# Conditioning rows by sums along the free axis, weights packed by tile, norms summed by a full matrix

## The chip, the cores and the metric

The kernel runs on one core of a Trainium2 chip. The metric is the device time of one execution in microseconds. Three runs of the kernel before took 2370.89, 2377.98 and 2380.05 us; their median is 2377.98 us.

## The reference

Two layers, each a mixer (eight heads of differential attention and eight heads of windowed grouped-query attention with a sink, side by side) and a squared-ReLU MLP, on 256 tokens of width 2048. Every sub-layer is modulated by a conditioning vector `c`:

```python
c_act = silu(c)
for layer in range(2):
    mod = c_act @ ada_w[layer] + ada_b[layer]           # 2048 -> 6 * 2048
    sh1, sc1, g1, sh2, sc2, g2 = split(mod, 6)
    h = rmsnorm(x, norm_mix[layer]) * (1 + sc1) + sh1
    proj = h @ w_in[layer]                              # 2048 -> 4608: qa, ka, va, qb, kb, vb
    ... two attentions ...
    x = x + g1 * (concat(out_a, out_b) @ w_out[layer])  # 2048 -> 2048
    h2 = rmsnorm(x, norm_mlp[layer]) * (1 + sc2) + sh2
    x = x + g2 * (square(relu(h2 @ w_up[layer])) @ w_down[layer])   # 2048 -> 8192 -> 2048
return rmsnorm(x, final_norm)
```

All is float32. `ada_w` alone has 201 MB, the other weights 377 MB, and each is read once.

## The kernel before

The activations stay in SBUF, transposed: `X[i]` holds two chunks of 128 features (partitions) by 256 tokens. Every weight comes from HBM as a tile `raw` of 512 KB (128 partitions x 1024 elements). ScalarE rounds it to `whi` (line 354, a cast to float32r), VectorE forms the rest `wlo = raw - whi` (line 355), and TensorE multiplies both with the two halves of the activation (lines 395 and 397 for most, 364 to 368 and 411 for others), so that a product is made of three, hi by hi, hi by lo and lo by hi. Layer 0's first pair of chunks stays whole (line 364).

The conditioning rows are a matrix-vector product of 201 MB, and VectorE makes it: `ada_job` loads tiles `araw` with the 2048 inputs on the partitions, 16 groups of 128 one after the other, multiplies each by its 128 values of `c_act` (one scalar a partition) and adds it to a running sum `ada` (lines 204 and 206, a `scalar_tensor_tensor` over 1024 columns). The 128 partitions of the sum are still to be added up: TensorE transposes it by the identity (line 213) and ScalarE copies each 128x128 block with `accum_out` (line 215); small VectorE operations add the bias and the norm's gain (lines 222, 225). One job makes up to eight rows of 128 values at once, after 16 groups.

`araw` and `raw` share one pool of six buffers of 512 KB (`rawp`). All loads stand on one queue, SyncE's, in the order of the program, and a load waits there until the buffer that it takes is free, that is until VectorE is done with the tile that lay in it. The `ada` tiles are dealt out between the weight tiles by `feed(rate)`, with rates in the tables `R0` to `R3`; `need` loads whatever is still missing when a row is used. A scheduler fixes the order on every engine before the run.

Around each sub-layer stands a norm. `square_sum` squares `X[i]` on ScalarE and sums over the partitions on TensorE with `mean_d`, a column of 1/2048, as the right operand (line 529, 16 matmuls with one column each); `rstd_cols` makes the reciprocal root of 2x128 values in nine small ScalarE operations (lines 537 to 545), and `spread` (line 552) brings it back on all partitions by a matmul with the identity. `modulated` (lines 590 to 604) then makes `h`. Nothing of the next product can start before that.

At the start `x` is loaded with tokens on the partitions and transposed by TensorE (line 294); at the end the result is transposed back (line 886), scaled and stored in eight pieces. The rotary tables (lines 309 to 348) are made after the first pair of chunks (`TAB = 0`).

Of the kernel before, what the change touches and what calls it, by code (L numbers as in the profile page):

```python
# [20 lines left out]
P = 128  # L21
S = 256
# [21 lines left out]
R0 = ([2.6, 1.4, 1.4, 0.8], 0.75, 1.0)  # L44
R1 = ([1.2, 0.2], 0.55, 0.65, 0.65)
R2, R3 = (0.75, 0.75, 0.75), (0.6, 0.6, 0.6, 0.6)
RATES = [dict(zip(("win", "qb", "wout"), R0)), R1, dict(zip(("win", "qb", "wout"), R2)), R3]
# [34 lines left out]

@with_exitstack
def encoder_trunk(
    ctx: ExitStack,
    tc: tile.TileContext,
    x, c, positions, ada_w, ada_b, norm_mix, w_in, diff_lambda, diff_subln,
    swa_sink, w_out, norm_mlp, w_up, w_down, final_norm, consts, out,
# [10 lines left out]
    adp = pool("adp", 1)  # L99
    tp = pool("tp", 5)  # L100
    ep = pool("ep", 4)
    wtp = pool("wtp", 3)
# [14 lines left out]
    def bslot(dt=F32R):  # L117

        return bp.tile([P, 2, 2, S], dt, tag="b", name=nm("b"))

# [21 lines left out]
    NV = 2 * NCH + DEPTH  # L142
# [3 lines left out]

    cstage = staged(P)[:NV, :]
    nc.sync.dma_start(cstage[:NCH, :], c[0].rearrange("(r q) -> r q", q=P))
    nc.sync.dma_start(cstage[NCH : 2 * NCH, :], final_norm.rearrange("(r q) -> r q", q=P))
    nc.sync.dma_start(cstage[2 * NCH :, :], diff_subln)  # L150
    ident = const_tile([P, P], "ident")
    nc.sync.dma_start(ident, consts[:, :P])
    xin = []
    for t in range(2):
        for hf in range(4):
            if hf % 2 == 0:
                xs = staged(1024)
            r = xs[:, (hf % 2) * 512 : (hf % 2 + 1) * 512]
            nc.sync.dma_start(r, x[0, t * P : (t + 1) * P, hf * 512 : (hf + 1) * 512])
            xin.append(r)  # L160
    mean_d = const_tile([P, 1], "mean_d")
# [5 lines left out]
    c15 = const_tile([P, 1], "c15")  # L167
    nc.vector.memset(c15, 1.5)
    halfpi = const_tile([P, 1], "halfpi")
    nc.vector.memset(halfpi, 0.5 * math.pi)  # L170


    pv = misc_bank()
    nc.tensor.transpose(pv[:, 0, :NV], cstage, ident[:NV, :NV])
    cvec = const_tile([P, NV], "cvec")
    nc.vector.tensor_copy(cvec, pv[:, 0, :NV])
    fin_g = cvec[:, NCH : 2 * NCH]
    c_act = const_tile([P, NCH], "c_act")
    nc.scalar.activation(c_act, cvec[:, :NCH], AF.Exp, scale=-1.0)
    nc.vector.tensor_scalar_add(c_act, c_act, 1.0)  # L180
    nc.vector.reciprocal(c_act, c_act)
    nc.vector.tensor_mul(c_act, c_act, cvec[:, :NCH])

# [731 lines left out]
```

## Time and profile before

| | |
|---|---|
| median of three runs | 2377.98 us |
| the profiled execution | 2371.55 us, of which the instructions span 2369.8 |
| PE busy | 2245.7 us, 95%, granted clock 0.977 on the mean |
| DVE busy | 1785.0 us, 75% |
| ACT busy | 1126.3 us, 48% |
| DMA | 586 MB, 247 GB/s on the mean, queue busy 73% |

PE is TensorE, DVE VectorE, ACT ScalarE, SPq the queue of loads and stores; "releaser" is what ended an engine's idle time. In time, the program is: start to 38 us; layer 0's mixer, `w_in` to about 265 (with the first heads near its end), heads to about 362, and the rest of the heads with `w_out` to 471; layer 0's MLP from 486 to 1247; layer 1's mixer from 1258 to 1627, whose `w_out` begins near 1540; layer 1's MLP from 1637 to 2358; the end. Between the parts stand norms. The `ada` tiles are all used by 1720 us.

### The profile page before, as it was taken

How to read it: one execution, taken by the hardware profiler on the slowest of the kernel's cores; microseconds unless marked ns; L12 is line 12 of the kernel's file. 1: busy time of each engine (PE TensorE's matmuls, PEld its weight loads, DVE VectorE, ACT ScalarE, POOL GpSimd, SP SyncE). 2: the span in 40 equal slices, each digit the busy share in tenths (PEclk: the TensorE clock that was granted, in tenths of full speed). 3: DMA queues.
4: the chain of work that ended last, by engine and by line, in shares of the span. 5: the costliest groups of instructions: out<-in, count | busy, mean ns of one | idle time of the engine just before them, and what ended most of it. 6: DMA issues, size and time to landing. Idle time of an engine off the chain costs nothing.

```text
span 2369.8 us, 34621 instructions
## 1 busy us (share of the span) xinstructions
PE 2245.7 (95%) x12883; PEld 1938.4 (82%) x12883; DVE 1785.0 (75%) x2356; ACT 1126.3 (48%) x1958; POOL 0.2 (0%) x4
## 2 busy tenths in 40 slices
PE   5888999889998999999998999998999999999998
PEld 3777887777887888888887887887888888888887
DVE  6899878988986768887778888899865454665453
ACT  4445665356443335444435557645454333444343
POOL 0000000000000000000000000000000000000000
PEclk7999999989999999999998999998999999999999
DMA  8998755889687888988885985586965556655553
GB/s 282 337 315 287 247 170 190 307 297 325 221 271 256 279 294 291 309 296 291 303 293 202 338 281 187 169 293 231 309 206 195 187 187 196 188 186 195 189 185 107
DMA packets 285612, 586.05 MB, mean 247 GB/s; under 512 B 22498, under 2 KB 31364, under 8 KB 285444
## 3 DMA queue, kind: packets, MB, share of 16 engines
q1 hardware_dynamic: 285444, 583.85, 73.0%
q8 instruction: 101, 1.65, 0.3%
q14 instruction: 67, 0.55, 0.1%
HBM read 581.66 MB, written 2.10 MB: 246 GB/s over the span
## 4 chain that ended last, share of the span: by engine, by line
PE 75%; DVE 10%; DMA 7%; ACT 4%; issue 3%; SPq 0%; DVEq 0%; ACTq 0%
PE acc L395 41%; PE acc L397 21%; DMA araw<-in_ada_w_dram 4%; DVE ada L206 3%; DVE wlo L355 3%; PE acc L368 2%; PE acc L367 2%; DMA raw<-in_w_in_dram 2%; PE acc L366 2%; PE lg L636 1%; ACT whi L354 1%; PE misc L621 1%; DVE x L756 1%; PE acc L364 1%; PE misc L529 1%
## 5 line engine op out<-in xcount | busy, mean ns | idle before, releaser
L395 PE MATMUL acc<-b,whi 128*128 128x512 f32 x4992 | 1760.7, 397 | 23.9 <-DVE x L756 11.2
L397 PE MATMUL acc<-b,wlo 128*128 128x256 f32 x4992 | 1393.1, 283 | 9.4 <-DVE wlo L355 9.2
L354 ACT CAST whi<-raw 128x1024 fp32r<-128x1024 f32 x711 | 725.1, 1049 | 903.0 <-PE acc L395 598.2
L395 PEld LDWEIGHTS acc<-b,whi 128*128 128x128 f32 x4992 | 935.6, 188 | 241.6 <-issue 18.3
L355 DVE TENSOR_TENSOR wlo<-raw,whi 128x1024 fp32r<-128x1024 f32 x711 | 851.2, 1221 | 350.0 <-ACT whi L354 345.0
L397 PEld LDWEIGHTS acc<-b,wlo 128*128 128x128 f32 x4992 | 947.1, 190 | 29.3 <-DVE wlo L355 17.3
L206 DVE SCALAR_TENSOR_TENSOR ada<-araw,c_act,ada 128x1024 f32<-128x1024 f32 (+1 forms) x375 | 464.6, 1239 | 111.3 <-DMA araw<-in_ada_w_dram 109.5
L756 DVE SCALAR_TENSOR_TENSOR x<-acc,mod,x 128x256 f32<-128x256 f32 x256 | 112.3, 479 | 15.1 <-PE acc L397 13.4
L366 PE MATMUL acc<-b,whi 128*128 128x256 f32 x320 | 91.7, 290 | 1.5 <-ACT whi L354 1.5
L367 PE MATMUL acc<-b,whi 128*128 128x256 f32 x320 | 90.7, 287 | 0.0
L368 PE MATMUL acc<-b,wlo 128*128 128x256 f32 x320 | 89.3, 289 | 0.9 <-DVE wlo L355 0.8
L474 ACT COPY tmp<-acc 128x256 f32<-128x256 f32 x120 | 44.3, 372 | 58.2 <-PE acc L397 57.8
L485 ACT CAST b<-tmp 128x512 fp32r<-128x512 f32 x72 | 44.7, 621 | 57.2 <-DVE tmp L844 55.0
L475 DVE TENSOR_TENSOR tmp<-tmp,acc 128x256 f32<-128x256 f32 x152 | 61.9, 417 | 12.1 <-ACT tmp L474 11.8
L366 PEld LDWEIGHTS acc<-b,whi 128*128 128x128 f32 x320 | 62.1, 194 | 2.9 <-ACT whi L354 2.1
L368 PEld LDWEIGHTS acc<-b,wlo 128*128 128x128 f32 x320 | 60.5, 193 | 3.2 <-issue 1.7
L367 PEld LDWEIGHTS acc<-b,whi 128*128 128x128 f32 x320 | 62.0, 194 | 1.1 <-issue 1.0
L367 PE MATMUL acc<-wlo,b 128*128 128x512 f32 (+1 forms) x152 | 56.4, 371 | 3.0 <-DVE wlo L355 3.0
L215 ACT ACTIVATE misc<-misc 128x128 f32<-128x128 f32 x192 | 50.0, 260 | 16.7 <-PE misc L213 15.0
L486 DVE TENSOR_TENSOR b<-tmp,b 128x512 fp32r<-128x512 f32 x72 | 49.1, 690 | 10.9 <-ACT b L485 9.3
L366 PE MATMUL acc<-whi,b 128*128 128x512 f32 (+1 forms) x152 | 54.1, 373 | 2.9 <-ACT whi L354 2.6
L368 PE MATMUL acc<-whi,b 128*128 128x512 f32 (+1 forms) x152 | 55.9, 368 | 0.0
(179 smaller groups left out, 1335.3 us busy)
## 6 DMA issues: line engine op xcount, KB each, us to landing
araw<-in_ada_w_dram SPq DMA_DIRECT2D x512, 256.0 KB, 5.0
raw<-in_w_up_dram SPq DMA_DIRECT2D x256, 512.0 KB, 4.7
raw<-in_w_down_dram SPq DMA_DIRECT2D x256, 512.0 KB, 4.5
raw<-in_w_in_dram SPq DMA_DIRECT2D x144, 512.0 KB, 5.3
araw<-in_ada_w_dram SPq DMA_DIRECT2D x128, 512.0 KB, 5.4
raw<-in_w_out_dram SPq DMA_DIRECT2D x64, 512.0 KB, 5.8
b<-in_x_dram SPq DMA_DIRECT2D x8, 256.0 KB, 4.5
out_dram<-tmp SPq DMA_DIRECT2D x8, 256.0 KB, 2.6
```

The lines of the kernel that those rows point to most:

```text
L206: nc.vector.scalar_tensor_tensor(acc, raw[:, j, :], cc, acc, op0=ALU.mult, op1=ALU.add)
L215: nc.scalar.activation(pm[:, t * P : (t + 1) * P], pm[:, t * P : (t + 1) * P], AF.Copy, accum_out=m[:, t0 + t : t0 + t + 1])
L354: nc.scalar.copy(hi, raw)
L355: nc.vector.tensor_tensor(lo, raw, hi.bitcast(F32), op=ALU.subtract)
L366: nc.tensor.matmul(o, lhsT=lhi, rhs=rhi, start=first, stop=False, skip_group_check=True)
L367: nc.tensor.matmul(o, lhsT=lhi, rhs=rlo, start=False, stop=False, skip_group_check=True)
L368: nc.tensor.matmul(o, lhsT=llo, rhs=rhi, start=False, stop=last, skip_group_check=True)
L395: nc.tensor.matmul(bank, lhsT=hi[:, fs], rhs=act[:, :, aj, :], start=first, stop=False, skip_group_check=True)
L397: nc.tensor.matmul(bank[:, 1, :], lhsT=lo[:, fs], rhs=act[:, 0, aj, :], start=False, stop=last, skip_group_check=True)
L475: nc.vector.tensor_add(tj, tj, b[:, 1, :])
L486: nc.vector.tensor_tensor(hl[:, 1], src, hl[:, 0].bitcast(F32), op=ALU.subtract)
L756: nc.vector.scalar_tensor_tensor(x[:, j, :], banks[2 * b + j][:, hf, :], g[j], x[:, j, :], op0=ALU.mult, op1=ALU.add)
```

## The change

1. `ada_w` is transposed on the host: a tile `araw` has 128 outputs on its partitions and 1024 of the 2048 inputs along the free axis. `c_act` is brought onto all partitions at the start (16 matmuls, line 221 after). One VectorE instruction, `tensor_tensor_reduce`, multiplies the tile by `c_act`, by a scale (the norm's gain, or 1), and adds along the row onto a starting value (the bias, then the first half's sum): 384 times, each followed by a second one that reads the sum out. The transposes, ScalarE's copies with `accum_out` and the small operations go; a chunk is ready after four tiles.
2. All weights are packed on the host so that a tile is one stretch of 512 KB in HBM, 4 KB a partition. Before, most rows of a tile had 2 KB.
3. `x` comes transposed and the result leaves transposed; TensorE's transposes at both ends go.
4. In the norm, `mean_d` is a full 128x128 matrix and the left operand, so that the sum stands on all partitions at once: six matmuls of 256 columns in place of 16, and no `spread`. Its arithmetic moves from ScalarE to VectorE: two ScalarE functions, then four VectorE operations over 128x256. `SQ_ADDED = 6`: six of the eight squares are added on VectorE first (before: four).
5. The tables are made after the fourth pair of chunks (`TAB = 3`). The `ada` tiles are paced by `GOALS`: how many are to be issued by the end of each part. `wtp` has two buffers for three.

```diff
-TAB = 0
+TAB = 3
-SLICES = {(0, 0): (256, 512, 512, 512, 256), (0, 3): (512,) * 4, (1, 0): (512,) * 4, (1, 3): (512,) * 4}
-R0 = ([2.6, 1.4, 1.4, 0.8], 0.75, 1.0)
...
+GOALS = [((72, 96, 120), (160, 204, 248, 304)), ((316, 326, 352), (384, 384, 384, 384))]
+SQ_ADDED = 6
...
+def tiled(w, blocks):
+    out = []
+    for c0, width in blocks:
+        for k, per in weight_tiles(c0, width, w.shape[0]):
+            t = w[k * P : (k + per) * P, c0 : c0 + width].reshape(per, P, width)
+            out.append(t.transpose(1, 0, 2).reshape(P, per * width))
+    return np.ascontiguousarray(np.stack(out))
...
-    def ada_job(l, sec, nsec, c0, width):
...
-                if k0 + j == 0:
-                    nc.vector.tensor_scalar_mul(acc, raw[:, j, :], cc)
+    def ada_job(l, rows):
+        for hf in range(2):
+            for sec, ch in rows:
...
+                raw = rawp.tile([P, RAW], F32, tag="raw", name=nm("araw"))
+                nc.sync.dma_start(raw, ada[l, sec, ch, hf])
...
-                    nc.vector.scalar_tensor_tensor(
-                        acc, raw[:, j, :], cc, acc, op0=ALU.mult, op1=ALU.add)
-        m = cp.tile([P, nt], F32, tag="mod", name=nm("mod"), bufs=28)
...
-                nc.tensor.transpose(pm[:, t * P : (t + 1) * P], acc[:, (t0 + t) * P : (t0 + t + 1) * P], ident)
-            for t in range(tn):
-                nc.scalar.activation(pm[:, t * P : (t + 1) * P], pm[:, t * P : (t + 1) * P], AF.Copy,
-                                     accum_out=m[:, t0 + t : t0 + t + 1])
...
+                nc.vector.tensor_tensor_reduce(
+                    raw, raw, c_act[:, hf * RAW : (hf + 1) * RAW], scale=scale,
+                    scalar=m[:, ch : ch + 1] if hf else vecs[:, b0 : b0 + 1], op0=ALU.mult, op1=ALU.add,
+                    accum_out=m[:, hf * NCH + ch : hf * NCH + ch + 1])
...
-            raw = rawp.tile([P, per, width], F32, tag="raw", name=nm("raw"))
-            nc.sync.dma_start(raw, wv[:, rows[u] : rows[u] + per, c0 : c0 + width])
+            raw = rawp.tile([P, RAW], F32, tag="raw", name=nm("raw"))
+            nc.sync.dma_start(raw, tiles[index[(c0, rows[u])]])
...
         for j in range(2):
-            for t in range(2):
-                nc.tensor.matmul(
-                    ssq[0][:, 0, t : t + 1], lhsT=sq[:, j, t * P : (t + 1) * P], rhs=mean_d,
...
+            nc.tensor.matmul(
+                ssq[0][:, 0, :], lhsT=mean_d, rhs=sq[:, j, :],
...
+    def norm_x():
+        ms = ssq[0][:, 0, :]
...
+        nc.scalar.activation(a, ms, AF.Ln, bias=eps)
         nc.scalar.activation(y, a, AF.Exp, scale=-0.5)
+        nc.vector.tensor_mul(a, y, y)
+        nc.vector.scalar_tensor_tensor(a, ms, EPS, a, op0=ALU.add, op1=ALU.mult)
+        nc.vector.tensor_scalar(a, a, -0.5, 1.5, op0=ALU.mult, op1=ALU.add)
+        nc.vector.tensor_mul(r, y, a)
...
+    for i in range(NCH // 2):
+        ot = tmp()
+        nc.vector.tensor_mul(ot, X[i], bc(rfin))
+        nc.sync.dma_start(out[i], ot)
```

The order on DVE before, at the norm that leads into layer 1's MLP (`wlo` a weight's rest, `ada` and `araw` a conditioning tile's sum and tile, `x_245` the last pair of chunks, L590 the first step of `h`):

```order
L756 SCALAR_TENSOR_TENSOR x_245<-acc_15267,mod_11790,x_245 128x256
L355 TENSOR_TENSOR wlo_15493<-raw_15490,whi_15492 128x1024
L355 TENSOR_TENSOR wlo_15531<-raw_15528,whi_15530 128x1024
L206 SCALAR_TENSOR_TENSOR ada_14918<-araw_15534,c_act,ada_14918 128x1024
L355 TENSOR_TENSOR wlo_15540<-raw_15537,whi_15539 128x1024
L206 SCALAR_TENSOR_TENSOR ada_14918<-araw_15581,c_act,ada_14918 128x1024
L590 TENSOR_TENSOR tmp_15403<-x_196,misc_15398 128x256 x2
```

And at the same place now; `x_107` is the last pair, L255 ISA the new product with, in the row behind it, the reading of its sum, L552 to L555 the norm's arithmetic, and L585 the first step of `h`:

```order
L761 SCALAR_TENSOR_TENSOR x_107<-acc_14360,mod_9619,x_107 128x256
L368 TENSOR_TENSOR wlo_14565<-raw_14562,whi_14564 128x1024
L255 ISA araw_14607,mod_14606<-araw_14607,c_act,vecs 128x1024
L255 ISA mod_14606 128x1
L368 TENSOR_TENSOR wlo_14571<-raw_14568,whi_14570 128x1024
L255 ISA araw_14654,mod_14606<-araw_14654,c_act,vecs 128x1024
L255 ISA mod_14606 128x1
L552 TENSOR_TENSOR b_14477<-b_14477 128x256
L368 TENSOR_TENSOR wlo_14613<-raw_14610,whi_14612 128x1024
L553 SCALAR_TENSOR_TENSOR b_14477<-misc_14354,b_14477 128x256
L368 TENSOR_TENSOR wlo_14619<-raw_14616,whi_14618 128x1024
L554 TENSOR_SCALAR b_14477<-b_14477 128x256
```

Behind these stand one more product with its reading, L555 and L585. So the norm's four operations now stand in VectorE's line, with two products and two weights' rests ahead of them, and two rests and a product between them, where before nothing of the norm was VectorE's.

On PE before, between two blocks of layer 0's MLP (`acc` sums of the block, `misc` the bank that takes the transposed conditioning sum):

```order
L395 MATMUL acc_6526<-b_6520,whi_6870 128x512
L397 MATMUL acc_6526<-b_6520,wlo_6871 128x256
L213 MATMUL misc_6910<-ident,ada_5678 128x128 x4
L213 MATMUL misc_6919<-ident,ada_5678 128x128 x4
L395 MATMUL acc_6937<-b_5731,whi_6943 128x512
L397 MATMUL acc_6937<-b_5731,wlo_6944 128x256
```

The rows L213 have gone from PE's line everywhere, and the L395 rows ahead of and behind them stand next to each other.

## Rows read from the trace of the kernel before

**Rows 1.** Windows by stage: length, PE, PEld, DVE, ACT, POOL, clock, DMA, GB/s.

```profile
0.00:38.00 38.00, 11.03 (x44) 8.70 (x45) 24.74 (x70) 15.79 (x46) 0.20 (x4) 0.74 0.87 270
38.00:265.00 227.00, 195.46 (x1205) 173.04 (x1205) 197.65 (x226) 108.69 (x203) 0.00 (x0) 0.94 0.91 315
362.00:471.00 109.00, 101.39 (x558) 82.11 (x555) 99.96 (x157) 46.96 (x100) 0.00 (x0) 1.00 0.77 261
486.00:661.00 175.00, 167.98 (x939) 144.18 (x939) 159.35 (x220) 94.42 (x172) 0.00 (x0) 0.98 0.84 282
661.00:1247.00 586.00, 572.55 (x3264) 496.83 (x3262) 448.91 (x494) 243.22 (x372) 0.00 (x0) 0.99 0.85 289
1300.00:1350.00 50.00, 48.99 (x226) 39.95 (x225) 42.47 (x45) 27.42 (x48) 0.00 (x0) 1.00 0.95 346
1540.00:1627.00 87.00, 83.12 (x484) 71.90 (x483) 82.35 (x113) 36.58 (x54) 0.00 (x0) 0.99 0.84 290
```

**Rows 2.** Groups by line: name, shapes, count, busy us, mean ns, idle before.

```profile
L355 DVE TENSOR_TENSOR wlo<-raw,whi 128x1024 fp32r<-128x1024 f32 x711 | 851.2, 1221 | 350.0 <-ACT whi L354 345.0 <-DMA raw<-in_w_out_dram 4.2
...
L206 DVE SCALAR_TENSOR_TENSOR ada<-araw,c_act,ada 128x1024 f32<-128x1024 f32 (+1 forms) x375 | 464.6, 1239 | 111.3 <-DMA araw<-in_ada_w_dram 109.5
...
L215 ACT ACTIVATION_READ_ACCUMULATOR misc<-misc 128x1 f32 x192 | 35.9, 187 | 0.0
...
L639 DVE TENSOR_REDUCE mx<-lg 128x2 f32<-128x512 f32 x32 | 21.9, 686 | 6.8 <-PE lg L636 6.8
```

**Rows 3.** Windows of line 206 alone: DVE busy us (count), clock, DMA share, GB/s.

```profile
38.00:265.00 227.00, 90.73 (x78) 0.94 0.91 315
362.00:471.00 109.00, 34.59 (x27) 1.00 0.77 261
486.00:661.00 175.00, 44.84 (x35) 0.98 0.84 282
661.00:1247.00 586.00, 147.60 (x115) 0.99 0.85 289
1540.00:1627.00 87.00, 25.57 (x20) 0.99 0.84 290
```

**Rows 4.** Windows of line 213 alone: busy us of PE and PEld (count).

```profile
486.00:1247.00 761.00, 9.53 (x72) 8.21 (x72) 0.99 0.85 287
1258.00:1720.00 462.00, 5.34 (x40) 4.68 (x40) 0.98 0.75 255
```

**Rows 5.** Waits, 38 to 265 us: engine, line, releaser, us, times, longest.

```profile
ACT whi L354 <- DMA raw<-in_w_in_dram: 65.4, 26, 7.0
```

**Rows 6.** Waits, 661 to 1247 us.

```profile
DVE ada L206 <- DMA araw<-in_ada_w_dram: 89.3, 58, 3.5
```

**Rows 7.** Timeline of DVE and PE at the start: start us, us, instruction, idle.

```profile
16.24 10.20 DVE L206 SCALAR_TENSOR_TENSOR ada<-araw,c_act,ada 128x512 f32<-128x512 f32 x13
...
37.78 9.36 PE L364 MATMUL acc<-b,raw 128*128 128x256 f32 x32 [3.88 <-ACT b L598]
```

**Rows 8.** Timeline of DVE and PE at the norm before layer 1's MLP.

```profile
1626.29 0.48 DVE L756 SCALAR_TENSOR_TENSOR x<-acc,mod,x 128x256 f32<-128x256 f32 x1
...
1633.25 0.75 DVE L590 TENSOR_TENSOR tmp<-x,misc 128x256 f32<-128x256 f32 x2 [0.69 <-ACT b L572]
...
1634.84 0.42 DVE L600 TENSOR_TENSOR b<-tmp,b 128x256 fp32r<-128x256 f32 x1
...
1635.41 0.77 PE L395 MATMUL acc<-b,whi 128*128 128x512 f32 x1 [2.60 <-DVE b L600]
```

**Rows 9.** Timeline of ACT at the end.

```profile
2357.28 0.63 ACT L517 ACTIVATE tmp<-x 128x512 f32<-128x512 f32 x1 [2.57 <-DVE x L756]
...
2365.61 0.69 ACT L889 ACTIVATE tmp<-acc,n 128x512 f32<-128x512 f32 x1 [0.74 <-DMA out_dram<-tmp]
```

**Rows 10.** DMA queue, 250 to 300, then 1850 to 1900 us: packets, MB, share.

```profile
q1 hardware_dynamic: 2907, 10.60, 63.8%
...
q1 hardware_dynamic: 4910, 9.47, 55.2%
```

More of the change, by code (lines that the diff above doesn't have):

```diff
@@ L80, in shape_constants, with weight_tiles, blocks_in, blocks_of @@
     return cst
+def weight_tiles(c0, width, rows):
+    per = max(RAW // width, 1)
+    return [(k, per) for k in range(0, rows // P, per)]
+def blocks_in(l):
+    w = 1024 if l == 0 else 512
+    out = [(c, w) for b in (KA, QA, QB) for c in range(b, b + 1024, w)]
+    return out + [(VA, 1024), (KB, 512)]
+def blocks_of(n):
+    return [(c, 512) for c in range(0, n, 512)]
+def tile_index(blocks, rows):
+    return {key: i for i, key in enumerate(
+        (c0, k) for c0, width in blocks for k, _ in weight_tiles(c0, width, rows))}
+def tiled(w, blocks):
[5 more added lines that the diff above has]
+    return np.ascontiguousarray(np.stack(out))
+def columns(*vectors):
+    return np.ascontiguousarray(
+        np.concatenate([np.asarray(v).reshape(-1, P).T for v in vectors], axis=1))
 @with_exitstack
@@ L119, in bslot, with single @@
         return bp.tile([P, 2, 2, S], dt, tag="b", name=nm("b"))
+    spare = []
+    def single():
+        if not spare:
+            pair = bslot(F32)
+            spare.extend((pair[:, 1], pair[:, 0]))
+        return spare.pop()
     def acc_bank():
@@ L716, in grouped_gemm @@
                 cap[0] = None if last else (*capped, k0 + gn + groups[gi + 1] - 1)
+            l0, s0 = capped or (0, 0)
+            r = pace(goal if last else 192 * l0 + 96 * (s0 // 3) + 4 * (k0 + gn + groups[gi + 1]),
+                     sum(width for _, width, _, _ in blocks) * gn // 1024)
             rows = list(range(k0, k0 + gn))
@@ L816, in mixer, with mlp @@
             blocks.insert(KV_AT[l], late[0])
-        grouped_gemm(w_in[l], blocks, groups, get_h, sliced["win"], (l, 1))
+        grouped_gemm(w_in[l], blocks, groups, get_h, goals[0], (l, 0))
         if KV_AT[l] >= 0:
             late.pop(0)
-        grouped_gemm(w_in[l], late, [NCH], get_h, sliced["qb"])
+        grouped_gemm(w_in[l], late, [NCH], get_h, goals[1])
+        rate = pace(goals[2], 32)
         for part in range(2):
-            acts = chunks_of(mixed[4 * part : 4 * part + 4])
+            acts = chunks_of(mixed[4 * part : 4 * part + 4], (l, part) not in WHOLE_MIXED)
             rows = list(range(8 * part, 8 * part + 8))
-            for nb in range(4):
-                banks = gemm(w_out[l], nb * 512, 512, rows, acts, "s", sliced["wout"])
-                residual(banks, l, 2, nb * 2, part == 1)
-    def mlp(l, groups, rates):
+            kind, w = ("f", 1024) if (l, part) in WHOLE_MIXED else ("s", 512)
+            for c0 in range(0, D, w):
+                banks = gemm(w_out[l], c0, w, rows, acts, kind, rate)
+                residual(banks, l, 2, c0 // (2 * P), part == 1, kind)
+    def mlp(l, groups, goals):
         with tc.high_priority():
```

313 lines of the change are left out of this document (132 added, 181 removed).

## The prediction, made before the changed kernel ran

> **What bounds the kernel now.** I read the windows by stage first [rows 1], because the mean over the span hides that the stages have different limits. From 38 to 265 us nothing has a margin: the transfer engines are busy 0.91 of the time at 315 GB/s, VectorE 197.65 of 227 us, TensorE 195.46, and ScalarE waits 65.4 us for weights of `w_in` [rows 5]. From 362 to 471 VectorE is the fullest of those that can't be overlapped, 99.96 of 109 us; in layer 1's `w_out`, 1540 to 1627, it has 82.35 of 87, or 0.947, which I take as the most that this engine reaches. In layer 0's MLP TensorE bounds: 167.98 of 175 and 572.55 of 586 us. There VectorE has room (448.91 of 586) and can even wait 89.3 us for conditioning tiles [rows 6]. After 1720 us no conditioning tile is left and nothing of the change falls there before the end. Then I read the groups by line [rows 2] for prices, the windows of single lines [rows 3, 4] for how much of each part lies in which stage, and the timeline at the start, at one norm and at the end [rows 7 to 9].
>
> All sums are made against the profiled execution, 2371.55 us; the median of the three runs is 6.4 us above it, and I add that at the end.
>
> **1. The start: -7 us.** Before, TensorE's first product starts at 37.78 us [rows 7], behind 14 half tiles of conditioning on VectorE (13 of them take 10.20 us), the transposes, ScalarE's sums and the tables. Now two chunks need eight tiles, and these with `x` and the vectors are some 6.5 MB; at the 270 GB/s of this stage [rows 1] that is 24 us, from 1 us on, so 25. Then come the last product (1.3), the norm's four operations over 256 columns (0.42 each as L600 has it, 1.7) and the 2.2 us that lie between the first step of `h` and the first matmul [rows 8]: 30.2. That is 7.6 less; I take 7. Bounds: 0, if `c_act`, which all products need, comes late behind 16 matmuls; -11, if the loads run at 315 GB/s.
>
> **2. The new product.** This instruction is in no row of before. Its nearest are two VectorE operations over two float32 operands of 1024 columns: 1.221 us (L355) and 1.239 on the mean (L206, the one that it replaces) [rows 2]. [...] The second instruction, which reads the sum, is bounded by 0 and by ScalarE's reading of its own, 0.187. Against L206 the pair costs between -0.02 and +0.17 us a tile; I take +0.10, about the middle, as a read of one column can't be free. What this does is worked out by stage, with the counts of [rows 3].
>
> 38 to 265: 78 x 0.10 = 7.8, and the tables move in from the head of the program (VectorE has 24.74 us in the first 38, 10.20 of them conditioning; of the other 14.5 I take half, 7). 197.65 + 14.8 = 212.5, while 0.947 of 227 is 215. So VectorE becomes the limit there, just as the faster loads could have shortened the stage. Term: 0. Bounds: -20, if VectorE isn't the limit and the loads run at the 346 GB/s that 1300 to 1350 shows (227 x (1 - 315/346)); +8, with 0.17 a tile and 222 us of work at 0.947.
>
> 362 to 471: the issue order has 25 tiles between the last of `w_in` and the last of `w_out`, where it had 32. 7 x 1.24 = 8.7 less, 25 x 0.10 = 2.5 more, two more additions of squares at 0.69 are 1.4: VectorE loses 4.8 and bounds here. Term: -5; bounds -8 and 0. The tiles left out fall due at the next norm, which is in point 5.
>
> 486 to 661: 159.35 + 3.5 = 162.9, under 0.947 x 175 = 165.7. Term 0; 0 to +2. 1540 to 1627, already at 0.947: 20 x 0.10 = +2; 0 to +4.
>
> **3. TensorE without the transposes: -15 us.** From 486 to 1247 they take 9.53 us of TensorE (72), from 1258 to 1720 5.34 (40) [rows 4], in stages where this engine is busy 96 to 98%. An instruction less in its line shortens them by its length: 14.9. In the first 486 us I count none of them, since TensorE waits there. Bounds: 0, if the places that they leave fill up with waits for weights, and -17. ScalarE loses its 192 copies too, but it is half idle, and I count nothing.
>
> **4. The layout in HBM, apart from the stage above: -4 us.** In 661 to 1247 TensorE is idle 13.45 us, mostly where VectorE stands at a conditioning tile that hasn't landed (the 89.3 us) and the weights behind it wait. Loads that land sooner give part of it; I take 4, with 0 and -13 as bounds. The row that should show what larger packets bring is mixed: between 250 and 300 us 2907 packets carried 10.60 MB (nearly all 4 KB) at 63.8% of the engines, which is 332 GB/s at full share; between 1850 and 1900, 4910 packets (nearly all 2 KB) carried 9.47 MB at 55.2%, 343 [rows 10]. So bytes, not packets, set the time. [...]
>
> **5. The norms: +4 us.** The arithmetic had ScalarE to itself and now stands in VectorE's line. Before layer 1's MLP, the last update of `x` ends at 1626.77 and TensorE resumes at 1635.41, 8.6 us later [rows 8]. Now two rests (1.22) and two products (1.34) stand ahead of L552, 5.1 us; then four operations at 0.42, and between them two rests and a product (3.8): 10.6 to the first step of `h`, and 2.2 from there to TensorE as before, 12.8. So +4. Before layer 1's mixer I get +1.5 in the same way (three rests and a product ahead, one rest between, 10.1). Before layer 0's MLP more conditioning tiles stand in the line, but there the gap of before is the longest, 471 to 486 us, and I get 13: -1.5. Together +4; bounds -2 and +8. What is queued behind L552 is only this norm's own and weights for products that wait for it, so nobody else pays.
>
> **6. The end: 0.** The last square begins at 2357.28 and takes 0.63. Two matmuls (32 take 9.36 us [rows 7], 0.3 each), two functions (under 0.63 each, I take 0.45), 4 x 0.42 and eight products over 512 columns, 0.69 each as L639's 512 columns, end at 2366.6; before, the last scaled piece ends at 2366.30 [rows 9]. The store behind is the same.
>
> **Sum:** -7 + 0 - 5 + 0 + 2 - 15 - 4 + 4 + 0 = -25. 2371.55 - 25 = 2346.5; with the 6.4 us to the median, **2353 us**. Taken within its own bounds this case lies between 2330 and 2366.
>
> **Rivals.** *Slower: the product with its sum is a slow instruction.* Place: VectorE, 38 to 265 us above all. At 0.45 us a tile more, that stage has 197.65 + 35 + 7 = 240 us of work, 253 at 0.947 (+26); 362 to 471 has +4, 486 to 661 185 for 175 (+10), 1540 to 1627 +9. That is 49, against -22 from the points that don't depend on it: +27, 2405. From about 0.36 a tile it decides for slower, from 0.27 it eats the gain. For it: nothing shows that the engine multiplies twice and adds along the row in one pass. [...] Its end is half rate: 1.07 us more and the 0.10, which by the same sum is +85, +22, +37, about +30 in 661 to 1247 and +25 in 1540 to 1627, with the -22 kept some +180: 2555. [...]
>
> *No change.* The product costs 0.20 to 0.36 more a tile and VectorE keeps in 38 to 265 and in layer 1's `w_out` what the transposes give: at 0.27 the stages lose 21 and the rest gives 22. 2377. For it: VectorE's 0.947 in 1540 to 1627. Against: the upper bound of 0.17 is below it.
>
> *A larger gain.* VectorE isn't a limit, since it stands idle for 29 of the 227 us from 38 to 265; the loads run at 346 GB/s there (-20) and layer 0's MLP loses its 13 idle us in place of 4. With the rest -54: 2324. For it: ScalarE's 65.4 us of waits for weights in 38 to 265; against: point 2's sum of VectorE's work.
>
> **How the numbers follow.** A difference of 0.5%, 12 us, is about what a measurement can tell from none here. Chances: my forecast 0.50, the larger gain 0.15, no change 0.19, slower 0.16 (0.09 near 2405, 0.07 up to half rate). Faster, below 2366: 0.46 of the first, 0.15 and 0.02 of the third, 0.63. Same: 0.04 of the first, 0.15 of the third, 0.19. Slower: 0.16 and 0.02 of the third, 0.18. The range goes from 2310, below the larger gain with some of its margin, to 2430, above the milder of the slow cases; half rate and a few per cent below are left out.
>
> **What would show it.** Right: the pair of the new product at 1.3 to 1.4 us; TensorE's first product near 30 us; VectorE above 93% to the end of `w_in`, at about the same time as before less the 7 us of the start; layer 0's MLP shorter by about 15; a gap of 12 us before layer 1's MLP. Wrong: the pair above 1.5 us, or a first stage that shortens by 20 us beyond the start with VectorE no fuller than now.

## The result, and the profile after

The changed kernel takes 2317.0 us (median of four runs, 2310.9 to 2330.5), the kernel before in the same session 2379.0. The ratio is 0.975, with an interval of 0.9725 to 0.9772: 62 us less, where 25 were forecast (2353 us). The profiled executions took 2371.55 and 2310.85 us, so that 60.7 us are to be found between two traces, each of one execution.

The table cuts both at the same events: TensorE's first product, the last matmul of layer 0's `w_in`, the start of the last square ahead of each norm, and the first product behind it.

| stretch | before | after | difference | forecast |
|---|---|---|---|---|
| start to the first product | 37.8 | 29.3 | -8.5 | -7 |
| layer 0's `w_in` and first heads | 303.5 | 303.1 | -0.4 | 0 |
| other heads and `w_out` | 132.7 | 120.1 | -12.6 | -5 |
| norm | 11.5 | 12.7 | +1.2 | -1.5 |
| layer 0's MLP | 761.3 | 731.6 | -29.7 | some -13 |
| norm | 8.7 | 10.0 | +1.3 | +1.5 |
| layer 1's mixer | 371.3 | 361.7 | -9.6 | some -2 |
| norm | 8.6 | 12.7 | +4.1 | +4 |
| layer 1's MLP | 721.9 | 714.9 | -7.0 | some -1 |
| last square to the end | 12.5 | 12.9 | +0.4 | 0 |

Windows of the changed kernel, in the columns of [rows 1]. The first three answer to its first three rows, shifted; the fourth is layer 0's MLP with the norm behind it, the last layer 1's MLP:

```profile
0.00:29.32 29.32, 10.08 (x45) 8.72 (x45) 18.81 (x45) 8.79 (x15) 0.20 (x4) 0.80 0.93 339
29.32:250.00 220.68, 190.10 (x1142) 166.86 (x1142) 195.16 (x289) 96.34 (x129) 0.00 (x0) 0.93 0.86 304
...
340.00:453.00 113.00, 105.76 (x592) 89.03 (x591) 109.27 (x213) 50.27 (x91) 0.00 (x0) 1.00 0.69 240
...
465.26:1206.83 741.57, 723.41 (x4109) 629.81 (x4109) 643.79 (x896) 322.16 (x395) 0.00 (x0) 0.99 0.86 309
...
1581.21:2296.13 714.92, 713.84 (x4104) 623.84 (x4104) 440.96 (x543) 306.89 (x377) 0.00 (x0) 1.00 0.62 203
```

The first stage is no shorter and VectorE hardly fuller (195.16 of 220.68 us, 0.884 where it was 0.871); its loads go at 304 GB/s where they went at 315. Layer 0's MLP has more VectorE work than before (643.79 us with the norm, 608.26 in [rows 1]) and is shorter. Groups by line, as in [rows 2]: the weights' rest, whose price is L355's, the new product, and the reading of its sum:

```profile
L368 DVE TENSOR_TENSOR wlo<-raw,whi 128x1024 fp32r<-128x1024 f32 x711 | 851.9, 1222 | 321.5 <-ACT whi L367 319.4
L255 DVE CUSTOM_DVE_ANT_0 araw<-araw,c_act,vecs 128x1024 f32<-128x1024 f32 x192 | 249.1, 1303 | 43.5 <-DMA araw<-in_ada_dram 43.3
L255 DVE CUSTOM_DVE_ANT_0 araw<-araw,c_act,mod 128x1024 f32<-128x1024 f32 x192 | 249.1, 1303 | 35.5 <-DMA araw<-in_ada_dram 35.1
...
L255 DVE DVE_READ_ACCUMULATOR2_ANT mod<- 128x1 f32 x384 | 33.1, 86 | 0.0
```

The first product, which answers to [rows 7], and the norm before layer 1's MLP, to [rows 8], in the timeline of DVE and PE:

```profile
29.32 1.22 PE L377 MATMUL acc<-b,raw 128*128 128x256 f32 x2 [3.81 <-ACT b L593]
...
1568.64 2.00 PE L541 MATMUL misc<-tmp,mean_d 128*128 128x256 f32 x8 [1.63 <-ACT tmp L530]
1569.36 1.28 DVE L255 CUSTOM_DVE_ANT_0 araw<-araw,c_act,vecs 128x1024 f32<-128x1024 f32 x1
...
1572.91 0.42 DVE L552 TENSOR_TENSOR b<-b 128x256 f32<-128x256 f32 x1
1573.24 1.22 DVE L368 TENSOR_TENSOR wlo<-raw,whi 128x1024 fp32r<-128x1024 f32 x1
1574.38 0.42 DVE L553 SCALAR_TENSOR_TENSOR b<-misc,b 128x256 f32<-128x256 f32 x1
...
1581.21 0.76 PE L408 MATMUL acc<-b,whi 128*128 128x512 f32 x1 [10.58 <-DVE b L595]
```

The norm's four operations stand between products and rests, as the order had it, and TensorE waits 10.58 us where it waited 2.60 at the same place. That term came as forecast. What was not in the forecast lies in the MLPs. Around 724 us the kernel before stops; PE, ACT and DVE there:

```profile
723.31 1.99 ACT L354 CAST whi<-raw 128x1024 fp32r<-128x1024 f32 x2 [3.66 <-PE acc L395]
723.93 1.03 PE L213 MATMUL misc<-ident,ada 128*128 128x128 f32 x8
725.21 0.26 ACT L215 ACTIVATE misc<-misc 128x128 f32<-128x128 f32 x1
...
727.33 1.28 DVE L206 SCALAR_TENSOR_TENSOR ada<-araw,c_act,ada 128x1024 f32<-128x1024 f32 x1
727.39 0.18 ACT L215 ACTIVATION_READ_ACCUMULATOR misc<-misc 128x1 f32 x1
728.53 0.16 DVE L222 TENSOR_TENSOR mod<-mod,vecs 128x8 f32<-128x8 f32 x1
...
729.85 3.22 DVE L756 SCALAR_TENSOR_TENSOR x<-acc,mod,x 128x256 f32<-128x256 f32 x8
731.26 0.77 PE L395 MATMUL acc<-b,whi 128*128 128x512 f32 x1 [6.29 <-DVE x L756]
```

Gates (the factors `g1`, `g2` of the reference) are needed for the update of `x`, and the update frees the banks that TensorE wants next. So the sums of a gate's rows go from TensorE (eight transposes, 1.03) to ScalarE, which has two casts ahead of them (its eight sums go from 725.21 to 727.57), to VectorE, which has a product ahead of the bias (728.53) and one more ahead of the update (729.85): 6.29 us. Behind them TensorE works at a lower clock: a window of 4 us has a granted clock of 0.51, and 12 matmuls, where the 4 us from 720 to 724 have 1.00 and 25, and 735.2 to 740 has 1.00 again:

```profile
731.20:735.20 4.00, 3.94 (x12) 3.39 (x13) 3.07 (x6) 0.00 (x0) 0.00 (x0) 0.51 0.83 320
```

In the changed kernel VectorE makes the gates alone, and from 575 to 1096 us no pair of matmuls is late. That the stop belongs to the chain (transposes, sums over rows, bias) is shown in the experiments.

A further part of the difference is seen in a place where nothing waits. Windows of 25 us, before and then after, TensorE busy throughout at the granted clock 1.00 (`x143` and `x146` behind TensorE's busy time are its matmuls):

```profile
775.00:800.00 25.00, 25.00 (x143) 21.69 (x142) 19.71 (x22) 7.99 (x8) 0.00 (x0) 1.00 0.83 285
```
```profile
775.00:800.00 25.00, 25.00 (x146) 22.05 (x145) 21.64 (x30) 8.09 (x9) 0.00 (x0) 1.00 0.87 300
```

143 matmuls against 146. The starts of the matmuls show why: a pair (512 columns by `whi`, 256 by `wlo`) takes on the mean either 0.3467 or 0.3533 us, and hardly anything between. (Single pairs vary, from 0.346 to 0.361 us in the long step; it is the mean over several that has two values: of 7527 means over twelve pairs in the two traces, 12 lie between 0.348 and 0.352 us.) I call them the short and the long step. A stretch without interruption keeps its step in these two traces: of the 88 that have eight pairs or more, the longest 1887, all but one do (before, 943.6 to 960.7 us). Counted over all such pairs, the profiled execution of the kernel before has 1859 in the long step, which cost 12.3 us, that of the changed kernel 466, 3.0 us. So 9.3 of the 60.7 us are this, 7.2 of them in layer 0's MLP. They are not shown to be the change's: what chooses the step isn't known (below), so they count as luck.

### The profile page after: what moved, and what is told of

The parts are those of the page before. It is cut to its first block, busy times and chain, and to the rows that moved or that the text cites. A ratio compares the mean times of both kernels' runs of the same rounds, so it can differ in the third digit from the quotient of the medians.

```text
span 2309.1 us, 33300 instructions
## 1 busy us (share of the span) xinstructions
PE 2191.3 (95%) x12540; PEld 1894.8 (82%) x12540; DVE 1808.1 (78%) x2698; ACT 1061.2 (46%) x1521; POOL 0.2 (0%) x4
## 4 chain that ended last, share of the span: by engine, by line
PE 83%; DVE 4%; ACT 2%; issue 1%; DMA 1%; ACTq 0%; DVEq 0%
PE acc L408 48%; PE acc L410 25%; PE acc L381 2%; PE acc L379 2%; PE acc L380 2%; PE misc L616 1%; DVE wlo L368 1%; PE lg L631 1%; DVE araw L255 1%; DVE x L761 1%; PE misc L608 1%; PE lg L680 1%; DMA raw<-in_w_up_dram 0%; ACT whi L367 0%; PE misc L562 0%
## 5 line engine op out<-in xcount | busy, mean ns | idle before, releaser
L408 PE MATMUL acc<-b,whi 128*128 128x512 f32 x4992 | 1742.5, 395 | 38.8 <-DVE b L595 29.4
L410 PE MATMUL acc<-b,wlo 128*128 128x256 f32 x4992 | 1377.1, 281 | 5.0 <-DVE wlo L368 4.8
L255 DVE CUSTOM_DVE_ANT_0 araw<-araw,c_act,vecs 128x1024 f32<-128x1024 f32 x192 | 249.1, 1303 | 43.5 <-DMA araw<-in_ada_dram 43.3
L255 DVE CUSTOM_DVE_ANT_0 araw<-araw,c_act,mod 128x1024 f32<-128x1024 f32 x192 | 249.1, 1303 | 35.5 <-DMA araw<-in_ada_dram 35.1
L381 PE MATMUL acc<-b,wlo 128*128 128x256 f32 x320 | 89.4, 293 | 2.5 <-DVE wlo L368 2.4
L530 ACT ACTIVATE tmp<-x 128x512 f32<-128x512 f32 x35 | 21.7, 631 | 75.7 <-DVE x L761 68.3
L381 PE MATMUL acc<-whi,b 128*128 128x512 f32 (+1 forms) x152 | 55.9, 367 | 0.0
```

What stands on the lines that cost most here:

```text
L255: nc.vector.tensor_tensor_reduce(raw, raw, c_act[:, hf * RAW : (hf + 1) * RAW], scale=scale, scalar=m[:, ch : ch + 1] if hf else vecs[:, b ...
L381: nc.tensor.matmul(o, lhsT=llo, rhs=rhi, start=False, stop=last, skip_group_check=True)
L408: nc.tensor.matmul(bank, lhsT=hi[:, fs], rhs=act[:, :, aj, :], start=first, stop=False, skip_group_check=True)
L410: nc.tensor.matmul(bank[:, 1, :], lhsT=lo[:, fs], rhs=act[:, 0, aj, :], start=False, stop=last, skip_group_check=True)
```

## The experiments

Which step a stretch has differs from kernel to kernel where the program is the same (layer 1's MLP, below), and the runs of one kernel lie up to 26 us apart. So each run is given twice: the median, and the span of its profiled execution less what its long steps cost. Neither is sharp: the medians come from sessions in which the kernel before lay between 2374.4 and 2381.7 us, and each span is of one execution, so differences of under some 7 us between whole kernels tell little.

| kernel | median (runs) | span | long steps | span less them |
|---|---|---|---|---|
| before | 2379.0 (4) | 2369.8 | 12.3 | 2357.5 |
| changed | 2317.0 (4) | 2309.1 | 3.0 | 2306.1 |
| b_packed | 2369.0 (10) | 2367.4 | 23.9 | 2343.5 |
| b_no_chain | 2363.1 (8) | 2361.0 | 23.1 | 2337.9 |
| b_packed_no_chain | 2348.9 (4) | 2344.1 | 21.2 | 2322.9 |
| w_rows | 2317.7 (4) | 2326.6 | 15.6 | 2311.0 |
| a_ada_2k | 2323.5 (6) | 2323.9 | 16.6 | 2307.3 |
| a_chain | 2364.4 (10) | 2359.2 | 7.9 | 2351.3 |
| a_transposes | 2363.4 (10) | 2356.4 | 17.9 | 2338.5 |
| a_wait | 2354.5 (6) | 2352.7 | 18.5 | 2334.2 |
| a_half | 2299.6 (2) | 2304.7 | 22.6 | 2282.1 |
| a_old_pacing | 2326.3 (4) | 2316.8 | 5.4 | 2311.4 |
| a_long_jobs | 2313.0 (6) | 2310.1 | 4.2 | 2305.9 |
| a_insert | 2319.3 (2) | 2313.8 | 2.9 | 2310.9 |
| a_better | 2321.0 (6) | 2318.2 | 11.6 | 2306.6 |
| a_norm3 | 2310.9 (6) | 2326.2 | 26.6 | 2299.6 |
| a_norm3_long | 2313.0 (6) | 2310.8 | 8.9 | 2301.9 |

**From the kernel before: packing and chain, alone and together.** b_packed loads every tile, weights and conditioning, as one packed stretch (the weights' line):

```diff
-            nc.sync.dma_start(raw, wv[:, rows[u] : rows[u] + per, c0 : c0 + width])
+            nc.sync.dma_start(raw.rearrange("p a b -> p (a b)"), w[0][w[1][(c0, rows[u])]])
```

> The kernel before, with every weight tile and every conditioning tile packed to one stretch of 512 KB, one DMA each; nothing else changed. Packing theory: 20 to 30 us faster than before, 2349 to 2359 us. Chain theory: 0 to 6 us faster, 2373 to 2379. The forecast had 4 us for this.

b_no_chain drops transposes and sums:

```diff
-                nc.tensor.transpose(pm[:, t * P : (t + 1) * P], acc[:, (t0 + t) * P : (t0 + t + 1) * P], ident)
...
-                                     accum_out=m[:, t0 + t : t0 + t + 1])
+        nc.vector.tensor_copy(m, acc[:, :nt])
```

> The kernel before, without the 192 transposes of the conditioning sums and ScalarE's 192 sums over their rows; one small VectorE copy takes a column of the sum instead, so that the rows are not the reference's values. Packing theory: the transposes cost their own length and no more, 12 to 15 us faster than before, 2364 to 2367. Chain theory: 30 to 40 us faster, 2339 to 2349, and the stall of TensorE of 6 us near 724 us and most of its slower stretches are gone from layer 0's MLP. The forecast had 15 us for this.

b_packed_no_chain has both edits.

> The kernel before with both edits of the two runs above together: all tiles packed, and no transposes and no ScalarE sums (a VectorE copy of a column stands for them, so the rows are not the reference's values). Alone they gave 9 and 15 us. Theory of two equal limits (TensorE's stalls behind the chain and VectorE's waits for conditioning tiles stand in for one another, so that taking one away leaves the other): more than the sum, 35 to 45 us faster than before, 2333 to 2343 us, and layer 0's MLP within 10 us of the changed kernel's 731. Additive theory: 24 us faster, 2354.

Ratios to before: 0.9968 (0.9942 to 0.9994), 0.9932 (0.9901 to 0.9964) and 0.9882 (0.9836 to 0.9927). By the medians 9, 15 and 29 to 33 us; by the spans less long steps 14, 20 and 35. So the two add up over the whole, and neither theory had the sizes: the packing is more than the forecast's 4 us and less than 20, the chain 15 to 20 and not 30.

Where they lie is another matter. Layer 0's MLP goes through two halves, each a `w_up` and a `w_down`. What each takes over its bare matmuls in the short step (177.5 us), less its long steps:

| kernel | first `w_up` | first `w_down` | second `w_up` | last `w_down` | sum |
|---|---|---|---|---|---|
| before | 15.5 | 10.1 | 6.5 | 11.5 | 43.6 |
| b_packed | 13.4 | 10.3 | 4.3 | 8.2 | 36.2 |
| b_no_chain | 12.3 | 2.4 | 9.8 | 17.6 | 42.1 |
| b_packed_no_chain | 12.6 | 1.1 | 5.3 | 10.4 | 29.4 |
| changed | 14.3 | 0.0 | 0.0 | 6.8 | 21.1 |

The first `w_down` holds the stop at 724 us. It loses 10 us in both kernels that have the chain (b_packed has the same stop, 6.29 us, too) and 1 to 2 in both that lack it: the stop is the chain's. But without the chain alone the second half gives nearly all of it back, 27.4 for 18.0: VectorE waits 103 us for conditioning tiles in this MLP, where it waited 89.3 [rows 6], and only the packing with it keeps the gain. So in this MLP b_no_chain wins 1.5 us. Most of its 20 lie ahead of it: its first matmul there starts at 471.7 us, 13.9 earlier than before (3.4 at the start, 2.3 in `w_in`, 6.3 in the heads with `w_out`, 1.9 in the norm).

**From the changed kernel: the layout undone.** w_rows reads the weights from the reference's own layout:

```diff
-            nc.sync.dma_start(raw, tiles[index[(c0, rows[u])]])
+            nc.sync.dma_start(
+                raw.rearrange("p (j c) -> p j c", c=width), tiles[:, rows[u] : rows[u] + per, c0 : c0 + width])
```

> The changed kernel, with all weights but the conditioning tiles read from the reference's own layout again (rows of 2 KB, of 4 KB in layer 0's w_in; the conditioning tiles stay packed). Packing theory (the 60 us come mostly from loads that land sooner): 20 to 30 us slower than the changed kernel, 2337 to 2347 us, most of it in layer 0's MLP and in layer 0's w_out. Chain theory (they come mostly from TensorE's and ScalarE's part in the conditioning rows, which is gone): 0 to 6 us slower, 2317 to 2323. The forecast had 4 us for this.

a_ada_2k loads each conditioning tile in two halves:

```diff
-                nc.sync.dma_start(raw, ada[l, sec, ch, hf])
+                for q in range(2):
+                    nc.sync.dma_start(raw[:, q * 512 : (q + 1) * 512], ada[l, sec, ch, hf][:, q * 512 : (q + 1) * 512])
```

> The changed kernel with each conditioning tile loaded as most were before, in two DMAs of 256 KB with rows of 2 KB (the tile itself and its use unchanged, weights packed). Packing all tiles of the kernel before gave 9 us in the medians and 14 in the profiled runs once the slower step of TensorE's stream is taken out; unpacking the weights alone cost the changed kernel nothing in the median and 5 in the same count. Theory that the conditioning tiles' loads carry the packing's gain: 7 to 12 us slower than the changed kernel, 2324 to 2329, VectorE's waits for these tiles in layer 0's MLP up from 37 to over 70 us. Rival, that the loads have slack there now: 2317 to 2320.

0.7 and 6.5 us by the medians, 5 and 1 by the spans: each is within what the runs scatter, and VectorE's waits for conditioning tiles in layer 0's MLP rise from 37.5 to 50.4 and 50.9 us only. So either half of the layout is worth 5 us or so once the chain is gone, and the theory that packing made the gain falls. Both halves undone together were not run.

**The chain put back.** a_chain adds two transposes and two sums behind each pair of rows; a_transposes the transposes alone; a_wait, in their place, two matmuls that wait for the same sum but read no tile:

```diff
+                        nc.tensor.transpose(pm[:, t * P : (t + 1) * P], raw[:, t * P : (t + 1) * P], ident)
...
+                        nc.scalar.activation(pm[:, t * P : (t + 1) * P], pm[:, t * P : (t + 1) * P], AF.Copy,
+                                             accum_out=col)
```
```diff
+                        nc.tensor.matmul(pm[:, t * P : (t + 1) * P], lhsT=mod[(l, sec, ch)].broadcast_to([P, P]),
+                                         rhs=ident, start=True, stop=True)
```

> The changed kernel, with a chain put back behind each pair of conditioning rows: two transposes of the product's tile by TensorE and two sums over rows by ScalarE, whose results are then used as the rows (so their values are not the reference's); 192 of each in all. Packing theory: 12 to 15 us slower than the changed kernel, 2329 to 2332. Chain theory: 30 to 40 us slower, 2347 to 2357. The forecast's price is 15 us.

> The changed kernel with the two transposes behind each pair of rows put back (192 in all, of the product's tile, so they wait for VectorE as before), but without ScalarE's sums: nobody reads them. The full chain cost 47 us in the medians. Theory that the hand-off costs (TensorE to ScalarE to VectorE, in each engine's line): the transposes alone cost their length, 192 x 0.09 to 0.11 = 17 to 21 us, 2334 to 2338. Rival, that TensorE waiting for VectorE's product is the cost: 40 us or more, 2357 and up.

> The changed kernel with two matmuls of 128 columns behind each pair of rows, by the column that VectorE has just summed and the identity: 192 in all, which wait for VectorE as the transposes did, but hold no conditioning tile; nobody reads them. The transposes of the tile alone cost 46 us in the medians, of which 17 to 21 is their length; there the queue of loads also waited 18.6 us in layer 0's MLP for transposes to release a tile. Theory that TensorE standing in line for VectorE is what costs: again about 45 us, 2355 to 2365. Rival, that the held tile was half of it: 20 to 28 us, 2337 to 2345, and the loads' queue waits for no such matmul.

47, 46 and 38 us by the medians, 45, 32 and 28 by the spans. Putting a chain in costs two to three times what taking it out gave: more than the packing theory's 12 to 15 us, and more than the chain theory's 30 to 40 too. It is not the chain of before, though: there the transposes read the running sum `ada`, which lies outside the buffers that the loads take, and here the product's own tile, which lies in one. The split into parts fails as well: a_transposes came out where its rival was, a_wait just below what it should then have been and above its rival, and a_wait was no clean test, as a float32 matmul of that kind stands twice in the records (384 for 192). In layer 0's MLP a pair with two transposes between takes 0.14 us longer, the same pair in a_wait 0.36; 44 groups make 6 and 16 us of the 18 and 26 that this stage loses, long steps apart. The held tile is a part in a_transposes, seen at the queue of loads, which waits for the transposes (in a_wait no such row stands):

```profile
SPq L248 <- PE misc L262: 18.6, 16, 3.5
SPq L455 <- PE misc L262: 14.3, 9, 2.5
```

What remains of either isn't settled, so the three runs say that such an insert is dear in the changed kernel, not what the chain cost before.

**VectorE as the limit.** a_half multiplies half of each tile:

```diff
-                    raw, raw, c_act[:, hf * RAW : (hf + 1) * RAW], scale=scale,
+                    raw[:, :512], raw[:, :512], c_act[:, hf * RAW : hf * RAW + 512], scale=scale,
```

> The changed kernel with the conditioning product over the first 512 of each tile's 1024 columns alone, all loads as they were: VectorE has some 0.65 us less per tile, 45 us less work up to the end of layer 0's w_in (the rows are then not the reference's). If VectorE limits that stretch, as the forecast had it: 15 to 30 us less there (303 us from the first product to the end of w_in, now). If loads or TensorE's own line limit it: under 6 us less. In layer 0's w_out, where the forecast had VectorE as the limit too: 5 us less, or none.

Windows from the first product to the end of `w_in`, then to the last square behind `w_out`, changed kernel and a_half:

```profile
29.32:332.40 303.08, 270.06 (x1664) 236.23 (x1665) 265.27 (x436) 151.78 (x264) 0.00 (x0) 0.94 0.80 281
332.40:452.50 120.10, 113.36 (x635) 95.23 (x633) 116.26 (x224) 55.84 (x98) 0.00 (x0) 1.00 0.71 244
```
```profile
29.42:316.90 287.48, 262.49 (x1664) 229.56 (x1665) 222.35 (x441) 151.74 (x264) 0.00 (x0) 0.97 0.83 300
316.90:432.10 115.20, 112.11 (x634) 95.43 (x633) 104.33 (x226) 55.57 (x99) 0.00 (x0) 1.00 0.74 250
```

43 us less of VectorE's work shorten the first by 15.6, 12 the second by 4.9. The same stretch takes 298 to 303 us in kernels with the same work (a_norm3 298.0, a_ada_2k 297.6), so 10 to 15 are the edit's, at or under the lower end of what was expected of VectorE as the limit and above the rival's 6. VectorE is a limit there though it is busy 0.875 of the time, by way of the loads: their queue waits 202 us of that stretch for VectorE to be done with a tile (lines 368 and 255), and with less work on VectorE ScalarE's waits for weights of `w_in` fall from 61.8 to 31.1 us.

**Pacing and jobs.** a_old_pacing deals the tiles out as before, a_long_jobs has jobs of eight rows:

```diff
-GOALS = [((72, 96, 120), (160, 204, 248, 304)), ((316, 326, 352), (384, 384, 384, 384))]
+GOALS = [((72, 93, 120), (166, 203, 244, 286)), ((331, 340, 364), (384, 384, 384, 384))]
```
```diff
-                queue.append(ada_job(l, [(sec + 1, ch), (sec, ch)]))
+                queue.append(ada_job(l, [(sec + s, ch + j) for s in (1, 0) for j in range(n)]))
...
```

> The changed kernel with only GOALS altered, so that as many conditioning tiles are issued by the end of each part as before (93, 128, 166, 203, 244, 286, 340, 364, 384). Theory that the shift of 32 tiles from layer 1's w_in into the MLPs, where VectorE and the loads have room, is a part of the gain: layer 1's mixer takes 368 to 371 us as before in place of 361.7, layer 0's MLP up to 3 us less than 731.6; 4 to 8 us slower than the changed kernel, 2321 to 2325. Rival, that the shift brings nothing: 2317, the mixer at 362.

> The changed kernel with jobs of 16 tiles and eight rows, as before, in place of four tiles and two rows, for all but the first rows of layer 0; every other thing as it is. Theory that the short jobs (a row is ready after two of its own tiles) are a part of the gain, what is left of it when chain, packing and pacing are counted (some 10 us, mostly in layer 0's MLP and w_out): 5 to 10 us slower, 2322 to 2327. Rival: 2317.

Pacing: 9 us by the medians, 5 by the spans, and not where the theory had it: the mixer takes 362.9, layer 0's MLP 740.9. The 18 tiles fewer there didn't help it, and why it is 9 us longer isn't known. Jobs: nothing (-4 by the medians, 0 by the spans); the theory falls.

**An insert alone.** a_insert puts eight transposes of the identity behind each block of layer 1's MLP.

```diff
+                        nc.tensor.transpose(pm[:, t * P : (t + 1) * P], ident, ident)
...
```

> The changed kernel with eight transposes of the identity on TensorE behind each of the 24 blocks of layer 1's MLP, whose results nobody reads: 192 in all, in a part where TensorE never waits. Theory that an insert costs its length alone: 24 x 0.9 = 21 us longer in that part (714.9 to 736), and the pairs of matmuls keep their distance of 0.347 us. Theory that an insert can leave the stream in its slower step: a share of the pairs, a third or more, goes at 0.353 us, which is up to 13 us on top, 736 to 749.

Half of them ran ahead of that part, since they wait for nothing and the scheduler moved them up. The 93 between its pairs lengthen it by 9.3 us, 0.79 a group of eight, 0.1 each, and 133 of 2009 steady pairs are long. In a_norm3, w_rows and a_ada_2k, with no insert, 1999 of 2027 are, in a_norm3_long none. So an insert cost 0.1 us a transpose here, and the long step comes without any insert; whether an insert can bring it on, one execution can't tell. Windows at the same place of a_norm3 and a_norm3_long:

```profile
1900.00:1925.00 25.00, 25.00 (x143) 21.69 (x142) 13.52 (x17) 7.99 (x8) 0.00 (x0) 1.00 0.58 189
```
```profile
1900.00:1925.00 25.00, 25.00 (x146) 21.87 (x145) 10.47 (x9) 9.98 (x10) 0.00 (x0) 1.00 0.60 194
```

**Versions meant to be better.** a_better has 16 more tiles in the first `w_up` (`GOALS`) and a shorter norm; a_norm3 the norm alone; a_norm3_long that and the long jobs.

```diff
-GOALS = [((72, 96, 120), (160, 204, 248, 304)), ((316, 326, 352), (384, 384, 384, 384))]
+GOALS = [((72, 96, 120), (176, 220, 264, 304)), ((316, 326, 352), (384, 384, 384, 384))]
...
-        nc.vector.tensor_mul(a, y, y)
-        nc.vector.scalar_tensor_tensor(a, ms, EPS, a, op0=ALU.add, op1=ALU.mult)
-        nc.vector.tensor_scalar(a, a, -0.5, 1.5, op0=ALU.mult, op1=ALU.add)
-        nc.vector.tensor_mul(r, y, a)
+        nc.vector.scalar_tensor_tensor(a, ms, EPS, y, op0=ALU.add, op1=ALU.mult)
+        nc.vector.scalar_tensor_tensor(a, a, -0.5, y, op0=ALU.mult, op1=ALU.mult)
+        nc.vector.scalar_tensor_tensor(r, a, 1.5, y, op0=ALU.add, op1=ALU.mult)
```

> The changed kernel with two edits: 16 conditioning tiles more in layer 0's first w_up (GOALS 176, 220, 264, 304), where the second half has none now and VectorE and the loads have room, so that 16 fewer stand in its last w_down, where 7 us are lost; and the norm's arithmetic in three VectorE operations for four (y times (1.5 minus half of m y y), the same value). If the places are read rightly: 4 to 5 us less in layer 0's MLP, and 0.4 to 1.5 less in each of four norms; 6 to 9 us faster than the changed kernel, 2308 to 2311. If the last w_down loses its time at the norm's squares and not to tiles: 2 to 4, 2313 to 2315.

> The changed kernel with the norm's arithmetic in three VectorE operations for four and nothing else (in the run with more tiles in the first w_up this took 1.4, 3.1, 0.4 and 0.3 us from the gaps before the three products and the end). 3 to 6 us faster than the changed kernel: 2311 to 2314. If the gaps are set by the conditioning products and weights' rests that stand in VectorE's line and not by the norm's own four: 0 to 2 us, 2315 to 2317.

> The same with the jobs of eight rows and 16 tiles, which alone gave 2313 us: 2308 to 2310 if both add, 2313 if one of the two was chance.

a_better's first `w_up` takes 11 us longer than the changed kernel's: it had no room. The three operations take 1.4, 0.3, 0.7 and 0.3 us from the gaps of a_norm3, 2.7 together, between the two expectations, and its median is 6 us lower, as the first of them had it; its span less long steps is 6.5 below the changed kernel's, its ratio to before, 0.9743 (0.9708 to 0.9779), can't be told from the changed kernel's. None of the three is shown to be faster.

## Why the prediction was wrong, point by point

1. The start: -7, measured -8.5. TensorE's first product stands at 29.32 us, 30.2 was worked out. Right; 3 of it come with the chain's removal alone (34.4 in b_no_chain).
2. The new product: 1303 ns and 86 for the reading; in layer 0's `w_in` a pair takes 1.29 us of VectorE (90.48 us for 70), L206 took 1.16 [rows 3], so +0.13, within the bounds. The rival of a slow instruction is out: 1024 columns take 1303 ns, 64 more than L206. No run shows the half rate at its end; the 1.07 us more that it supposes is, as an estimate from [rows 2], what 1024 columns cost there, twice what lies between L355's 1221 ns and L639's 686 for 512. The bounds of -0.02 and +0.17 take the product at L355's price, and no row of before shows that adding along the row adds nothing to that: it took 82 ns more. The first stage's term of 0 came (-0.4, though kernels of the same work have up to 5 less), and a_half shows VectorE's work as a limit, but not by being full: the 93% that should show it were 88%. The stage's upper bound of +8 doesn't follow from its terms: 197.65, 13.3 and 7 make 218 and not 222 us of work, and so +3. For 362 to 471 us I had -5 and a bound of -8; it is -12.6 with the heads ahead of it. VectorE's work in that stretch fell by the 4.8 that were summed (121.02 to 116.26 us), but 0.947, which I took as the most that this engine reaches, isn't: it was busy 0.912 of the stretch before and is 0.968 now. b_no_chain has -6.3 of it, and ScalarE's waits for `w_out` fall, as the waits of before and after show from the end of `w_in` to the update:

```profile
ACT whi L354 <- DMA raw<-in_w_out_dram: 32.8, 18, 3.8
```
```profile
ACT whi L367 <- DMA raw<-in_w_out_dram: 13.3, 4, 5.5
```

3. This is the step that failed: "An instruction less in its line shortens them by its length", with two things put at nothing beside it, "In the first 486 us I count none of them, since TensorE waits there" and "ScalarE loses its 192 copies too, but it is half idle, and I count nothing". The chain gave 15 by the medians and 20 by the spans alone, so the 15 look right, but that is luck: their places are others. Ahead of layer 0's MLP, where nothing was counted, 64 transposes take 10.6 us of TensorE in the kernel before, and b_no_chain gains 13.9 there; inside that MLP, where 9.5 were counted, it gains 1.5. What was left out is who waits for the result. The rows come to VectorE through three engines' lines, and where a gate is the last thing missing, as at 724 us, TensorE stands for 6.29 us and is then granted 0.51 of its clock for some 4; that gain shows only when the loads are faster too. Chain and packing together gave 29 to 35 where I had 19. An instruction's length was no more than I had it: 0.1 us for a transpose in a steady stream, 0.13 in my sum.
4. The layout: -4. By itself 9 to 14 before, some 5 or less in the changed kernel. So this term was too small for the kernel before, and the idle time that it rests on was misread: of TensorE's 13.45 us not most lay behind conditioning tiles, as 6.29 are the stop at 724 us and 3.8 stand at the norm's squares and an update of `x`. w_rows, with 2 KB in most weights, is at 0.7 us by the medians and 5 by the spans, too near to nothing to show what such rows cost.
5. The norms: +4 in all, the three gaps and the end measured +7. The gap before layer 1's MLP is as worked out (12.9 from the last update, 12.8 forecast), that before layer 0's is not 1.5 shorter. But a gain was left out, the norm's sum on TensorE. It had 20 one-column matmuls a norm (five tiles of four, not the 16 of the section on the kernel before), 5.82 us with layer 0's MLP and the norm behind it; six of 256 columns take 3.02. Layer 1's last `w_down`, where no conditioning tile is left, shows what this is worth: less long steps it takes 4.9 us over its bare matmuls in all four kernels with the old norm, and 3.0 in all with the new one but a_insert, whose inserts stand there. That is 1.9 a norm, some 8 over four.
6. The end: 0, measured +0.4.

The largest miss is layer 0's MLP, -29.7 for -13. By their places 7 are the transposes' length, 8 the stop at 724 us with its slow matmuls, 7.2 the long steps, 2 the norm's sum; some 5 remain for waits that I can't assign. The long steps were no term of mine, nor of any rival. The rival of a larger gain had nearly the right time (2324), but by luck: the first stage gave none of its 20 us. Between b_packed_no_chain and the changed kernel 17 us of span less long steps remain: 5 are the start, some 5 may be pacing (a_old_pacing), the norms' gaps take 7 back, and some 14 lie in `w_out` and the MLPs, read from the stretches and not tested.

Of the 36 us between the forecast's 25 and the 60.7 of the traces, then, 9 are long steps, some 12 the chain and the layout beyond their 19 (3 more stand in the start), and some 8 the norm's sum at nothing; the start has 1.5 more, the norms take 3 more back, and some 8 stay open.

## What to carry to other kernels

A result that goes through three engines can cost more than its instructions where it is made just in time (6.29 us at one place here): look for the place where its last consumer frees what the busiest engine waits for, and price the stop there. Taking a part away from one kernel and putting something like it into another measure different things (15 to 20 us for b_no_chain, 45 to 47 for a_chain), and a gain can vanish at one place while another limit stands (1.5 us in layer 0's MLP for b_no_chain, 14.2 with packing): run each edit alone and both together, and compare place by place. Compare the rate of a stretch without waits in two traces before a difference is put down to the change.

## What was not expected of the hardware

TensorE's steady stream of pairs runs at 0.3467 or at 0.3533 us a pair, both at granted clock 1.00 and with TensorE busy 25.00 of 25 us. In layer 1's MLP, whose products are the same in all kernels, nine of the 17 profiled executions have 1600 or more of some 2030 steady pairs in the long step (up to 13.3 us), the other eight 360 or fewer; what chooses it stays open. VectorE's product with its sum over 1024 columns takes 1303 ns and over 512 columns 767 (a_half); by these two, an estimate, that is about 1.05 ns a column and 0.23 us besides. A transpose of 128x128 put between two matmuls of a steady stream lengthens it by 0.1 us, though its record says 0.27 (a_insert, groups of eight; 0.07 in a_transposes' pairs).
